# A streaming encoder step: first unit of the out-projection transposed among the value and gate blocks, two tanh buffers, one more mixer step, first sums of the up projection queued behind out-projection operands

## Chip, core and metric

One core of a Trainium2 chip runs the whole program. The metric is the device time in microseconds of one launch. Engine names are those of the profile: PE multiplies matrices (PEld is its weight load), DVE and ACT do elementwise work, POOL is the general engine, SP issues most DMAs.

## The reference

One layer of a hybrid encoder takes 1024 new frames of one stream (the prompt) and 32 frames of a running stream (the samples), each of 1024 channels. Three groups of heads mix along time, each with a state that is carried from chunk to chunk of 64 frames; then come an out-projection and a feed-forward part with a causal convolution.

```python
proj = xn @ w_in                      # xn = rms_norm(x); 15 pieces
# GLA, 6 heads, and HGRN2, 5 heads, per chunk of 64:
scores = jnp.einsum('bihd,bjhd,bijhd->bijh', qc, kc, decay)
o = (jnp.einsum('bijh,bjhv->bihv', scores, vc)
     + jnp.einsum('bihk,bhkv->bihv', qc * jnp.exp(b), s))
# mLSTM, 5 heads: the same with stabilised weights and a normaliser
cat = jnp.concatenate([o_a, o_b, o_c], axis=-1)   # normed per head, times a gate
h = cat @ w_out
x = x + rms_norm(h, g_mix_post)
up, buf = causal_dwconv(rms_norm(x, g_ffn_pre) @ w_up, ...)
x = x + rms_norm((gelu(gate) * val) @ w_down, g_ffn_post)
```

All of it is in fp32. The states and the convolutions' last rows are outputs too.

## The kernel before

Every fp32 product is made of three matmuls on operands that are split into a high and a low half (`mm3`, L100 to L103): high by high, high by low, low by high. So each operand has an "h" tile, which ACT casts, and an "l" tile, which the DVE subtracts.

*In-projection.* Frames come in three groups of 384, 384 and 288 (256 of the prompt and the 32 samples). For each group `inproj` first makes feature blocks (tiles pf, 24 matmuls each), then value and gate blocks (tiles pv). In the last group a block of 256 columns is made in two halves of 128 (`vg_across`, L446 to L474): ACT copies each half out of PSUM (vf, L468), and PE transposes it back (pb, L455). Gates go through `vg_store` (L415 to L432): tanh on ACT into the tile vth (L113), one or two DVE operations (L427, L429), a multiply on POOL (L431), and a DMA.

*Mixers.* A unit is 128 frames; unit 8 is the 32 samples. `mixer` (L719 to L1027) is a generator with NMIX = 11 steps: it loads the unit's queries and keys (qkb, L729), makes the decayed queries qe on ACT (L812), the operands Qz and Ld of the scores on the DVE, the scores on PE (sc, L717), puts them into P (L805), and sums og, oh, om and oi on PE (all L717; mi are small sums); the DVE brings these into the tile cat (L990), POOL multiplies it with the gate (L992), and it is stored (L1025). og needs P, oi comes after om, and each PSUM bank is free again when its cat is made.

*Interleaving.* `merge(main, nmain, nside)` runs the main generator and after each of its steps as many steps of the mixers as keep both in proportion. So NMIX and nmain shift every mixer step among the main work. A scheduler then orders the instructions of each engine; `tc.high_priority` pulls an instruction ahead and `tc.issue_after` holds one behind another. Each engine runs its own list in order.

*Out-projection.* `outproj(u)` (L1054 to L1187) loads a unit's cat (tile ct), transposes it (ctp, L1074), splits it (ch on ACT L1078, cl on DVE L1079), multiplies it with the weights (zp), squares and copies the result on ACT (L1101, L1102), norms it, adds the residual and transposes it for the next stage (fxt). `out_weights` casts the eight rows of w_out (woh on ACT, L107 and L1048; wol on the DVE, L110 and L1050). They come through a ring of seven tiles of which six are loaded first. `pipeline` (L1191) runs the units 0, 1, 2, 3, 8, 4, 5, and the mixers of 8, 6 and 7 run beside it. Units 6 and 7 follow by hand, beside the start of the up projection.

*Up projection.* `col_operands` (L1211 to L1243) splits sums of blocks of the normed activations xg0 into B21h, B21l, B11h and so on (ACT L1221, DVE L1222). The weights come as wu0r and wu22r, and ACT casts them into A_0h and S_0h.

## Time and profile before

| | us |
|---|---|
| median of three runs | 1377.05 |
| their range | 1376.05 to 1380.32 |
| the profiled execution | 1379.03 |
| its span in the trace | 1377.3 |
| PE busy | 1313.3 |
| DVE busy | 1031.8 |
| ACT busy | 703.9 |
| POOL busy | 325.6 |

A row of the timeline gives the start, the duration, the engine, the line, the operation with its output and inputs, and in brackets how long the engine stood idle before it and what ended that. The granted clock of PE is a column of the view by stretches (1.00 is full speed).

### The profile page before, as it was taken

How to read it: one execution, taken by the hardware profiler on the slowest of the kernel's cores; microseconds unless marked ns; L12 is line 12 of the kernel's file. 1: busy time of each engine (PE TensorE's matmuls, PEld its weight loads, DVE VectorE, ACT ScalarE, POOL GpSimd, SP SyncE). 2: the span in 40 equal slices, each digit the busy share in tenths (PEclk: the TensorE clock that was granted, in tenths of full speed). 3: DMA queues.
4: the chain of work that ended last, by engine and by line, in shares of the span. 5: the costliest groups of instructions: out<-in, count | busy, mean ns of one | idle time of the engine just before them, and what ended most of it. 6: DMA issues, size and time to landing. Idle time of an engine off the chain costs nothing.

```text
span 1377.3 us, 29190 instructions
## 1 busy us (share of the span) xinstructions
PE 1313.3 (95%) x11472; PEld 1194.7 (87%) x11472; DVE 1031.8 (75%) x1916; ACT 703.9 (51%) x1368; POOL 325.6 (24%) x529
## 2 busy tenths in 40 slices
PE   6999999998998989997989999999999999999996
PEld 5999989998887877866879999999999997678885
DVE  4786469668597577796778888888888875499566
ACT  4555556554474554443575455455555445454552
POOL 5532403145122064133111112121121110010005
PEclk9999999999999999999999999999999999999998
DMA  9599869785888844534323565645474239744435
GB/s 343 203 321 359 288 235 299 267 281 188 273 256 309 303 147 161 155 114 151 110 77 110 170 165 135 163 129 163 111 182 126 81 114 390 290 153 136 146 106 123
DMA packets 125825, 269.72 MB, mean 196 GB/s; under 512 B 24007, under 2 KB 59367, under 8 KB 125607
## 3 DMA queue, kind: packets, MB, share of 16 engines
q1 hardware_dynamic: 111959, 245.43, 52.2%
q0 software_dynamic: 8928, 18.09, 7.2%
q10 hardware_dynamic: 4800, 4.33, 0.9%
q8 instruction: 90, 1.47, 0.4%
q14 instruction: 48, 0.39, 0.1%
HBM read 206.72 MB, written 86.18 MB: 213 GB/s over the span
## 4 chain that ended last, share of the span: by engine, by line
PE 72%; DVE 11%; DMA 7%; ACT 5%; issue 2%; POOL 2%; SPq 1%; ACTq 0%; DVEq 0%; POOLq 0%
PE pux L103 5%; PE pux L101 5%; PE pux L102 5%; PE puw L101 3%; PE puw L102 3%; PE puw L103 3%; PE pv L101 3%; PE pv L103 3%; PE q L101 3%; PE pv L102 3%; PE q L102 3%; PE q L103 3%; PE x L101 2%; PE x L102 2%; PE x L103 2%
## 5 line engine op out<-in xcount | busy, mean ns | idle before, releaser
L1368 DVE SCALAR_TENSOR_TENSOR y<-uu,fconv_sb,y 128x1060 f32<-128x1060 f32 x88 | 116.2, 1320 | 37.3 <-ACT y L1366 36.9
L1304 ACT COPY c<-pux 128x272 f32<-128x272 f32 (+1 forms) x132 | 49.4, 376 | 48.3 <-PE pux L103 47.6
L101 PE MATMUL zp<-woh,ch 128*128 128x512 f32 (+1 forms) x144 | 60.5, 422 | 4.8 <-ACT ch L1078 2.8
L101 PE MATMUL pv<-wt_0h,xh 128*128 128x256 f32 (+2 forms) x195 | 57.6, 296 | 5.2 <-ACT xh L321 2.8
L103 PE MATMUL zp<-woh,cl 128*128 128x512 f32 (+1 forms) x144 | 59.0, 410 | 1.9 <-DVE cl L1079 1.9
L1366 ACT ACTIVATE y<-uu,fconv_sb 128x1060 f32<-128x1060 f32 x44 | 56.0, 1273 | 7.9 <-POOL uu L1362 6.8
L102 PE MATMUL zp<-wol,ch 128*128 128x512 f32 (+1 forms) x144 | 58.9, 409 | 0.0
L1365 POOL COPY fhalo<-uu 128x2 f32<-128x2 f32 x44 | 16.5, 376 | 178.9 <-DVE uu L1309 178.7
L103 PE MATMUL pv<-wt_0h,xl 128*128 128x256 f32 (+2 forms) x195 | 56.0, 287 | 0.2 <-DVE xl L322 0.2
L102 PE MATMUL pv<-wt_0l,xh 128*128 128x256 f32 (+2 forms) x195 | 56.0, 287 | 0.1
L103 PE MATMUL pv<-wt_1h,xl 128*128 128x256 f32 (+2 forms) x195 | 56.1, 288 | 0.0
L101 PE MATMUL pv<-wt_1h,xh 128*128 128x256 f32 (+2 forms) x195 | 55.9, 287 | 0.0
L102 PE MATMUL pv<-wt_1l,xh 128*128 128x256 f32 (+2 forms) x195 | 55.7, 286 | 0.0
L1544 POOL TENSOR_TENSOR gss<-gss 128x1 f32<-128x1 f32 (+1 forms) x9 | 8.4, 930 | 185.1 <-ACT gjk L1537 185.1
L220 POOL TENSOR_SCALAR hrs<-hss 128x5 f32<-128x5 f32 (+3 forms) x27 | 9.7, 358 | 175.4 <-DVE hss L988 174.7
L805 DVE COPY_PREDICATED P<-masks_sb,sc 128x352 f32<-128x352 int32 (+3 forms) x53 | 37.8, 714 | 11.6 <-PE sc L717 10.9
L101 PEld LDWEIGHTS pv<-wt_0h,xh 128*128 128x128 f32 (+1 forms) x195 | 36.8, 189 | 7.1 <-ACT xh L321 3.5
L431 POOL TENSOR_TENSOR vg<-vth,gh 128x256 f32<-128x256 f32 (+1 forms) x36 | 29.1, 810 | 58.5 <-DVE vth L427 36.6
L221 POOL TENSOR_TENSOR hrs<-hrs,mhalf 128x5 f32<-128x5 f32 (+3 forms) x27 | 39.7, 1471 | 2.2
L827 ACT ACTIVATE x<-x 128x256 f32<-128x256 f32 (+1 forms) x44 | 17.9, 406 | 43.3 <-DVE x L825 36.1
L101 PEld LDWEIGHTS zp<-woh,ch 128*128 128x128 f32 (+1 forms) x144 | 27.4, 190 | 12.5 <-ACT ch L1078 3.0
L992 POOL TENSOR_TENSOR cat<-cat,gt 128x320 f32<-128x320 f32 (+3 forms) x27 | 31.7, 1174 | 26.4 <-DVE cat L990 26.3
(1714 smaller groups left out, 5351.3 us busy)
## 6 DMA issues: line engine op xcount, KB each, us to landing
wrP<-in_w_dn SPq DMA_DIRECT2D x27, 512.0 KB, 4.0
h_d<-y SPq DMA_DIRECT2D x22, 530.0 KB, 3.2
ht<-h_d SPq DMA_DIRECT2D x22, 530.0 KB, 9.8
wt_0r<-in_w_tok SPq DMA_DIRECT2D x21, 512.0 KB, 7.1
wt_1r<-in_w_tok SPq DMA_DIRECT2D x21, 512.0 KB, 6.1
ws_d<-in_w_dn POOLq DMA_DIRECT2D x20, 512.0 KB, 9.1
wrP<-ws_d SPq DMA_DIRECT2D x20, 512.0 KB, 3.9
wt_0l<-lt_d SPq DMA_DIRECT2D x14, 512.0 KB, 5.7
```

The lines of the kernel that those rows point to most:

```text
L101: pe.matmul(ps, lh[0], rh[0], start=first, stop=False, **kw)
L102: pe.matmul(ps, lh[0], rh[1], start=False, stop=False, **kw)
L103: return pe.matmul(ps, lh[1], rh[0], start=False, stop=last, **kw)
L221: pool.tensor_tensor(out, out, mhalf[:n, :cols], op=ALU.pow)
L431: pool.tensor_tensor(o[:n], th[:n], gh[:n, c0:c0 + 256], op=ALU.mult)
L805: dve.copy_predicated(dst, mk.broadcast_to([n, 11, *mk.shape[2:]]), src)
L827: act.activation(xv[:, :, 0, :], xv[:, :, 0, :], AF.Exp, scale=-1.0)
L992: pool.tensor_tensor(cat[:n, c0:c0 + 64 * nh], cat[:n, c0:c0 + 64 * nh], gt[:n, c0:c0 + 64 * nh], op=ALU.mult)
L1304: kept[name] = act.copy(t, ps)
L1365: behind["POOL"] = pool.tensor_copy(fhalo[:, j, :], u[:, NCOL - 2:NCOL])
L1366: act.activation(y, u, AF.Identity, scale=fconv[:, j, 2:3], bias=fconv[:, j, 3:4])
L1368: dve.scalar_tensor_tensor(y, uu[i][:, s:s + NCOL], fconv[:, j, s:s + 1], y, op0=ALU.mult, op1=ALU.add)
```

## The change

1. Unit 0's transposes and halves are started inside `vg_across`, after the first half of the last block, with tiles of their own in a pool pc0; `pipeline` no longer starts unit 0, and unit 1's cat is loaded after unit 0's transposes.
2. vth has two buffers, in the pool of the in-projection, which the weights of the out-projection take over later.
3. ACT's copy vf is made with high priority.
4. The mixer has one more step ahead of og (NMIX 12, and `merge` gets 25 instead of 26 for the pipeline).
5. xg0 is allocated later, in the memory that pc0 leaves.
6. B21's halves of the first block are held behind the last ch and cl of unit 7.

Numbers of instructions stay nearly the same on every engine. What the order shows:

ACT at the start of the out-projection, before. ch with 6872 and 6881 are unit 0's halves, vth with 6836, 6842 and 6848 the last tanhs, qe is unit 6's.

```order
L468 COPY vf_6745<-pv_7_1_6801 128x288
L113 ACTIVATE vth_7_6836<-pb_7_6827 128x256
L107 CAST woh<-wor_5736 128x1024
L107 CAST woh<-wor_5738 128x1024
L1078 CAST ch_6872<-ctp_6867 128x512
L113 ACTIVATE vth_7_6842<-pb_7_6827 128x256
L1078 CAST ch_6881<-ctp_6876 128x512
L1048 CAST woh<-wor_5740 128x1024
L1048 CAST woh<-wor_5742 128x1024
```

And of the change, the same place, from the same copy vf on:

```order
L469 COPY vf_6748<-pv_7_1_6822 128x288
L113 ACTIVATE vth_7_6857<-pb_7_6848 128x256
L113 ACTIVATE vth_7_6863<-pb_7_6848 128x256
L113 ACTIVATE vth_7_6869<-pb_7_6849 32x256
L819 ACTIVATE qe_7397<-qkb_7336,cf_sb 128x128 x4
L995 ACTIVATE sq_0_7234<-og_7189 32x384
L107 CAST woh<-wor_5736 128x1024
L107 CAST woh<-wor_5738 128x1024
L1056 CAST woh<-wor_5740 128x1024
```

ch of unit 0 has moved ahead of this piece, all tanhs and qe of unit 6 stand ahead of the first cast of the weights, and so does a square of og of unit 8 (sq). Before, qe stood behind the last cast.

PE at unit 6's om and oi in the change (zp with 7773 is the second half of unit 3; 24 of its products stand ahead of om):

```order
L103 MATMUL zp_7773<-woh,cl_7665 128x512
L724 MATMUL om_7800<-vm_157,w_7405 64x65 x10
L724 MATMUL oi_7801<-C_0_7747,mqz 64x65
L724 MATMUL oi_7801<-C_1_6498,mqz 64x65
L724 MATMUL oi_7801<-C_0_7747,mqz 64x65
```

Before, the same om stood among the products of unit 8's second half (zp with 8284), 30 products after og:

```order
L103 MATMUL zp_8284<-woh,cl_7847 32x512
L717 MATMUL om_7770<-vm_157,w_7375 64x65 x10
L101 MATMUL zp_8284<-woh,ch_7846 32x512
L102 MATMUL zp_8284<-wol,ch_7846 32x512
L103 MATMUL zp_8284<-woh,cl_7847 32x512
```

There 18 products of zp_8284 and the four transposes of the next unit stood between om and oi; now nothing does.

ACT at the end of unit 5 in the change (zp with 8485 and 8512 are unit 5's halves, ch with 8567 and 8576 unit 6's, with 8612 and 8620 unit 7's):

```order
L1115 COPY z_8484<-zp_8485 128x512
L1238 CAST B11h_8766<-xg_8628 128x1088
L107 CAST A_0h<-wu0r 128x512 x2
L1114 ACTIVATE z_8484,oss_8483<-zp_8512 128x512
L107 CAST A_0h<-wu22r 128x512
L1115 COPY z_8484<-zp_8512 128x512
L1086 CAST ch_8567<-ctp_8562 128x512
L1086 CAST ch_8576<-ctp_8571 128x512
L1086 CAST ch_8612<-ctp_8607 128x512
```

Before, at the same place:

```order
L987 ACTIVATE sq_11_8373<-hn_8365 128x320
L1221 CAST B21h_8758<-xg_6864 128x1088
L1101 ACTIVATE z_8485,oss_8484<-zp_8513 128x512
L1221 CAST B11h_8762<-xg_6864 128x1088
L1102 COPY z_8485<-zp_8513 128x512
L1078 CAST ch_8568<-ctp_8563 128x512
L1078 CAST ch_8577<-ctp_8572 128x512
L1078 CAST ch_8613<-ctp_8608 128x512
L107 CAST A_0h<-wu0r 128x512 x2
```

B21h is gone from the front and follows the last ch; the three casts A_0h now stand ahead of unit 6's ch.

The diff:

```diff
...
     cols_of, dcs_of = {}, {}
     HSET = (2, 0, 4, 5)
     VGD = (lambda b, h: b > 0, lambda b, h: True, lambda b, h: True)
-    pws, wo_raw, ring = ExitStack(), [], []
+    pws, pcs, wo_raw, ring, p2, wo, opened = ExitStack(), ExitStack(), [], [], [], [], []
     NRING, CT0 = 7, 6
 
     ct_of, xr_of, tail, xlate, mixed = {}, {}, [], {}, set()
...
                 act.dma_start(v_d[t:t + n, 256 * blk:256 * blk + 256], o[:n])
                 return
             c0 = 256 * (blk - 4)
-            th = mx.tile([128, 256], F32, tag="vth", name=f"vth{u}_{blk}", bufs=1)
+            th = p1.tile([128, 256], F32, tag="vth", name=f"vth{u}_{blk}", bufs=2)
             ia = tanh(th[:n], ps[:n, :256], 0.5)
             ns = min(max(704 - c0, 0), 256)
             if ns:
...
                     ps = psb.tile([128, T], F32, tag="big", name=f"pv{g}_{blk}_{e}")
                     for k in range(8):
                         mm3(ps, [w[:, 128 * e:128 * e + 128] for w in ws[k]], (xh[:, k, :], xl[:, k, :]), k == 0, k == 7)
-                    act.copy(fs[e], ps)
+                    with tc.high_priority(offset=AHEAD):
+                        act.copy(fs[e], ps)
+                    if blk == blks[-1] and not e:
+                        first = outproj(RING[0])
+                        next(first)
+                        next(first)
+                        opened.append(first)
                     if before and not e:
                         back(*before)
                     yield
...
                     load_cat(0)
                 wo_raw.append(ring[0](f"wor{k}"))
                 sp.dma_start(wo_raw[k], a["w_out"][k])
+            p2.append(pcs.enter_context(tc.tile_pool(name="pc0", bufs=1, side="left")))
         if sl:
             yield from vg_across(range(1, 8))
             return
...
             if last_pair:
                 put(0, sd[:n].unsqueeze(2).broadcast_to([n, 11, cl]))
             yield
+        yield
 
         og = psm.tile([128, 6, 64], F32, tag="o", name=f"og{u}", bufs=2)
         oh = psm.tile([128, 5, 64], F32, tag="o", name=f"oh{u}", bufs=2)
...
     lev_index = {16: 0, 8: 1, 4: 2, 2: 3, 1: 4, 0: 5}
 
 
-    def outproj_setup(p2):
-        woh = p2.tile([128, 8, 1024], F32R, name="woh")
-        wol = p2.tile([128, 8, 1024], F32R, name="wol")
-        gm = p2.tile([128, 1024], F32, name="gm")
+    def outproj_setup():
+        woh = p2[-1].tile([128, 8, 1024], F32R, name="woh")
+        wol = p2[-1].tile([128, 8, 1024], F32R, name="wol")
+        gm = p2[-1].tile([128, 1024], F32, name="gm")
         sp.dma_start(gm, a["grows"][0:1, :].broadcast_to([128, 1024]))
         return gm, woh, wol
 
...
             yield
 
 
-    def outproj(p2, W, u):
-
-        gm, woh, wol = W[:3]
+    def outproj(u):
+
         n = 128 if u < 8 else DEC
         t0 = 128 * u
         load_cat(u)
-        if u in RING:
+        if u in RING[1:]:
             load_cat((RING + (6,))[RING.index(u) + 1])
         ct = ct_of[u]
         chs = []
...
             for k in range(4):
                 c = 512 * hf + 128 * k
                 pe.transpose(ps[:, k, :n], ct[:n, c:c + 128], ident[:n, :n])
-            ch = p2.tile([128, 4, 128], F32R, tag="ch", name=f"ch{u}{hf}", bufs=3)
-            cl = p2.tile([128, 4, 128], F32R, tag="cl", name=f"cl{u}{hf}", bufs=3)
+            own = f"{hf}" if u == RING[0] else ""
+            ch = p2[-1].tile([128, 4, 128], F32R, tag="ch" + own, name=f"ch{u}{hf}", bufs=1 if own else 3)
+            cl = p2[-1].tile([128, 4, 128], F32R, tag="cl" + own, name=f"cl{u}{hf}", bufs=1 if own else 3)
             with tc.high_priority(offset=AHEAD):
                 ins = (act.copy(ch[:, :, :n], ps[:, :, :n]),
                        dve.tensor_tensor(cl[:, :, :n], ps[:, :, :n], ch[:, :, :n].bitcast(F32), op=ALU.subtract))
             if u == RING[0]:
                 halves[:] = ins
+            if u == 7:
+                kept["ch"], kept["cl"] = ins
             chs += [(ch[:, k, :n], cl[:, k, :n]) for k in range(4)]
             if u in RING:
                 yield
         if u not in RING:
             yield
+        if u == RING[0]:
+            load_cat(RING[1])
         if u in RING:
             load_res(u)
-        ss = p2.tile([128, 4], F32, tag="oss", name=f"oss{u}", bufs=2)
+        gm, woh, wol = wo[:3]
+        ss = p2[-1].tile([128, 4], F32, tag="oss", name=f"oss{u}", bufs=2)
         cs = [slice(512 * hf, 512 * hf + 512) for hf in range(2)]
 
         def bank(hf):
...
 
             pss = [bank(hf) for hf in range(2)]
             for k in range(8):
-                next(W[3])
+                next(wo[3])
                 for hf in range(2):
                     product(pss[hf], hf, k)
             z = ring[0](f"z{u}")
...
             zt = z[:, :8 * n].rearrange("p (k n) -> p k n", n=n)
         else:
             s = u > 5
+            if not s and 0 not in xlate:
+                pcs.close()
+                xlate[0] = p3s.enter_context(tc.tile_pool(name="p3", bufs=1, side="right")).tile([128, 8, 2, SUBS[0][1]], F32, name="xg0")
             o = fcol(u) - HW - SUBS[s][0] - 2
             zt = xlate[s][:, :, 1, o:o + n]
         for hf in range(2):
...
     def pipeline(gens):
 
 
-        next(gens[0])
-        next(gens[0])
-        yield
         for i, x in enumerate(gens):
             after = gens[i + 1:i + 2]
             next(x)
...
             h = p.tile([128, 4, n], F32R, name=f"{name}h{s}")
             l = p.tile([128, 4, n], F32R, name=f"{name}l{s}")
             res[name] = h, l
-            act.copy(h, src)
-            return dve.tensor_tensor(l, src, h.bitcast(F32), op=ALU.subtract)
+            with ExitStack() as late:
+                if s == 0 and name == "B21":
+                    late.enter_context(tc.issue_after(kept["ch"].ins))
+                    late.enter_context(tc.issue_after(kept["cl"].ins))
+                act.copy(h, src)
+                return dve.tensor_tensor(l, src, h.bitcast(F32), op=ALU.subtract)
 
         halves("B21", q["B21"])
         halves("B11", q["B11"])
...
         return chain_of(*[mixer(u, g, c) for (u, c) in us[-1:] + us[:-1]]) if us[-1][0] == 8 else \
             chain_of(*[mixer(u, g, c) for (u, c) in us])
 
-    NMIX, NIN = 11, 12 + 2 + 24
+    NMIX, NIN = 12, 12 + 2 + 24
 
     for g in range(3):
         xs_ = norm_tiles(g)
...
         side.append(mixers(g))
     p1s.close()
     p2s = ExitStack()
-    p2 = p2s.enter_context(tc.tile_pool(name="p2", bufs=1, side="right"))
-    wo = outproj_setup(p2)
-    wo += (out_weights(wo),)
+    p2.append(p2s.enter_context(tc.tile_pool(name="p2", bufs=1, side="right")))
+    wo += outproj_setup()
+    wo.append(out_weights(wo))
     p3s = ExitStack()
 
-    x0 = p3s.enter_context(tc.tile_pool(name="p3", bufs=1, side="right")).tile([128, 8, 2, SUBS[0][1]], F32, name="xg0")
-    xlate[0] = x0
     n0, n1 = SUBS[0][1], SUBS[1][1]
     smp = DEC // 2
-    firsts = [outproj(p2, wo, u) for u in RING]
-    merge(pipeline(firsts), 26, 3 * NMIX + 2)
+    firsts = opened + [outproj(u) for u in RING[1:]]
+    merge(pipeline(firsts), 25, 3 * NMIX + 2)
     pump(1000)
-    last = [outproj(p2, wo, u) for u in (6, 7)]
+    last = [outproj(u) for u in (6, 7)]
     for x in (last[0], last[0], last[1]):
         next(x)
+    if 0 not in xlate:
+        pcs.close()
+        xlate[0] = p3s.enter_context(tc.tile_pool(name="p3", bufs=1, side="right")).tile([128, 8, 2, SUBS[0][1]], F32, name="xg0")
+    x0 = xlate[0]
     sp.dma_start(x0[:, :, 0, :], xn_d[:, :, 0:n0])
     sp.dma_start(x0[:, :, 1, :smp], xn_d[:, :, HW:HW + smp])
     sp.dma_start(x0[:, :, 1, smp:smp + 128], xn_d[:, :, fcol(4):fcol(5)])
```

## The prediction

> **What bounds the kernel now.** The page first: PE is busy almost the whole span.
>
> ```profile
> PE 1313.3 (95%) x11472; PEld 1194.7 (87%) x11472; DVE 1031.8 (75%) x1916; ACT 703.9 (51%) x1368; POOL 325.6 (24%) x529
> ```
>
> Only 64.0 us (1377.3 less 1313.3) are open on PE, so an edit that adds no products can win little. I then read what PE waited for between 480 and 710 us, where most of the edits lie (us in total, times, longest).
>
> ```profile
> PE zp L101 <- ACT ch L1078: 2.8, 1, 2.8
> PE sc L717 <- DVE Qz L839: 1.5, 1, 1.5
> PE pb L455 <- DVE vth L427: 1.3, 1, 1.3
> PE ctp L1074 <- ACT vth L113: 0.8, 1, 0.8
> PE pv L101 <- DVE vth L427: 0.8, 2, 0.6
> ```
>
> No wait is long, and three groups answer to the edits: the tanh buffer (pb, pv, ctp), the operands of unit 6 (ch), and the waits of mixers. The table by stretches adds the clock: in the first 8 us of the out-projection it is half, so products cost twice.
>
> ```profile
> 514.00:522.00 8.00, 2.51 (x4) 1.33 (x4) 0.50 0.96 347
> 645.00:654.00 9.00, 3.83 (x24) 2.68 (x23) 6.53 (x8) 6.28 (x11) 4.13 (x5) 0.89 0.56 173
> ```
>
> The columns are busy PE and PEld (the second row all five engines), then the clock and the DMA share; the first row counts L102 alone, of which only the clock is used. In the second, PE works 3.83 of 9 us: that is the densest loss in the kernel.
>
> **Term A, two tanh buffers.** The tanh tile had one buffer, so a new tanh waits until POOL has read the last one. The trace of this tile and PE's rows:
>
> ```profile
>   POOL vg L431: 21.5, 15
> 338.39 0.40 PE L101 MATMUL pv<-wt_0h,xh 128*128 128x282 f32 x1 [1.35 <-ACT vth L113]
> 493.05 0.38 PE L455 MATMUL pb<-ident,vf 128*32 128x128 f32 x2 [1.27 <-DVE vth L427]
> ```
>
> ACT stood 21.5 us in 15 waits for POOL, but of that only 1.35, 1.3 and 0.8 us came through to PE (3.4 us), and 0.8 more to ctp. A second buffer takes away exactly this wait. ACT's high priority for the vf copy costs no instruction; it matters only where PE waits for the copy, and I count it at nothing, bounds 1 us either way. What is late next is POOL's own multiply, which is not faster.
>
> **Term B, one more step in each mixer.** The order puts one block of 24 products more between a mixer's last sum (mi) and og for unit 3, whose og waited:
>
> ```profile
> 316.33 0.92 PE L717 MATMUL og<-v,P 64*64 64x64 f32 x24 [2.81 <-DVE P L805]
> 506.03 0.29 PE L102 MATMUL pv<-xl,wt_1h 128*128 128x288 f32 x1
> 506.16 0.29 PE L103 MATMUL pv<-xh,wt_1l 128*128 128x288 f32 x1
> ```
>
> Products of this kind start 0.13 us apart, so 24 of them are 3.1 us, more than the 2.81. The price is that blocks elsewhere in the mixer lose cover; no row shows such a wait, so I bound it by the same 2.8 us of loss. A and B together offer 6.2 us. Because each stage still has the DVE behind it, I take half, **−3.1 us**, with bounds −7 and +3.
>
> **Term C, the start of the out-projection.** T is the end of the value and gate products, 506.4 us by the row above. Unit 0's eight transposes and its four halves stand ahead of T now. That alone would let unit 0 begin early. But its first product also needs the cast weights woh, and the order puts qe of unit 6 ahead of all eight casts on ACT. ACT's rows before, with the load of qkb on SP, the first product, and the last scores, og and oh of unit 8:
>
> ```profile
> 509.80 0.42 PE L717 MATMUL sc<-cf_sb,x 128*32 128x11 f32 x8
> 517.19 1.48 PE L717 MATMUL og<-v,P 32*32 32x64 f32 x12
> 531.47 0.86 PE L717 MATMUL og<-S,qz 128*32 128x64 f32 x12
> 532.16 0.72 PE L717 MATMUL oh<-S,qz 128*32 128x64 f32 x10
> 509.08 1.98 ACT L107 CAST woh<-wor 128x1024 fp32r<-128x1024 f32 x2
> 513.42 4.83 ACT L1048 CAST woh<-wor 128x1024 fp32r<-128x1024 f32 x5
> 516.52 0.84 SPq L729 DMA_DIRECT2D qkb<-qkb_d  x2
> 522.50 1.28 ACT L812 ACTIVATE qe<-qkb,cf_sb 128x128 f32<-128x128 f32 x4 [3.05 <-DMA qkb<-qkb_d]
> 513.93 0.76 PE L101 MATMUL zp<-woh,ch 128*128 128x512 f32 x1 [1.04 <-issue]
> 532.86 0.69 DVE L1079 TENSOR_TENSOR cl<-ctp,ch 128x512 fp32r<-128x512 f32 x1 [9.24 <-ACT ch L1078]
> ```
>
> Before, the casts begin at T+2.7 and the first product at T+7.5. After, SP issues qkb when unit 8's scores are over, T+3.8 by the first row, say T+4. From issue to qe took 6.0 us (516.52 to 522.50), so qe runs from T+10 to T+11.3; one square and one cast of 1.0 us (1.98 for two) follow, and the first product stands near T+13: 5.5 us later. Against that stand og and oh of unit 8, 3.1 us of PE (1.48, 0.86 and 0.72), which the order puts ahead of the first product and thus into this hole. Unit 0's products stay spread by the casts and the DVE's subtractions (five took 5.77 us), and the eighth cast, behind a load which is now queued after qkb, may hold its last six. I take **+2 us**. The DVE's idle 9.24 us before 532.86 is what unit 6's mixer may use, since its qkb is now there early: if all its work falls there the start wins 3 us. The upper end is a late load: qe of unit 7 waited 9.4 us for its qkb, and with that much more for qkb, and some 4.6 us more for the eighth cast's load behind it, the end is +16. The wait, in the view of ACT's waits:
>
> ```profile
> ACT qe L812 <- DMA qkb<-qkb_d: 12.5, 2, 9.4
> ```
>
> PE will idle 6 us there, and the clock goes with it: in the row of 514 to 522 it was 0.50 after idle pieces of about 1 us. The Trainium skill, "TensorE: Matmul & The Clock Gate", Part 1: The HAM clock gate, says that the array returns to half speed after an idle window of about 3.4 us and recovers after a busy one. By that rule one more window at half speed may follow, an estimate of 1.7 us more; this trace halves the clock with far smaller gaps, so the hole does not have to add any, and the sum goes without it.
>
> **Term D, units 6 and 7 among the products.** Both mixers stand half a unit to one and a half earlier among the products (og half a unit, the first scores more). Before, unit 7 paid at its end:
>
> ```profile
> 626.54 0.91 PE L717 MATMUL og<-v,P 64*64 64x64 f32 x24 [0.93 <-DVE P L805]
> 628.71 0.76 PE L717 MATMUL oh<-S,qz 128*64 128x64 f32 x20
> 632.35 0.80 PE L717 MATMUL om<-vm,w 64*64 64x65 f32 x20 [1.83 <-DVE cat L990]
> 631.74 0.56 DVE L990 TENSOR_TENSOR cat<-og,hrs 128x384 f32<-128x384 f32 x1 [0.68 <-POOL hrs L221]
> 539.00 2.44 DVE L781 TENSOR_TENSOR qz<-qkb,eb 32x256 f32<-32x256 f32 x6
> 633.27 0.49 DVE L990 TENSOR_TENSOR cat<-oh,hrs 128x320 f32<-128x320 f32 x1 [0.18 <-POOL hrs L221]
> ```
>
> Now 22 products stand ahead of unit 7's og and 23 ahead of its om, some 5 us each, so these 2.76 us go. For unit 6 it is worse: oi follows om directly, and the DVE has the decay, four query products and the solver's operands of unit 7 ahead of the cat that frees oi's bank. In the rows above that cat ends at 633.76, 4.3 us after the last product of og and oh (628.71 and 0.76). The query products alone took 2.44 us for unit 6; with the rest I estimate 4, which makes 8.3. The cover is 24 products 0.23 us apart (5.5 us, by two rows of the next fence) and om, 0.80: 6.3 us. So oi waits 2.0 us: D is 2.0 − 2.8 = **−0.8 us**, bounds −2.8 and +6 (unit 7's qkb as late as above).
>
> **Term E, unit 6's operands ahead of B21's halves.** ACT, SP and PE at the end of unit 5:
>
> ```profile
> 644.59 0.39 PE L102 MATMUL zp<-wol,ch 128*128 128x512 f32 x1
> 644.82 0.40 PE L103 MATMUL zp<-woh,cl 128*128 128x512 f32 x1
> 647.30 1.10 ACT L1221 CAST B21h<-xg 128x1088 fp32r<-128x1088 f32 x1 [3.56 <-POOL cat L992]
> 648.89 1.09 ACT L1221 CAST B11h<-xg 128x1088 fp32r<-128x1088 f32 x1
> 650.36 1.57 ACT L1078 CAST ch<-ctp 128x512 fp32r<-128x512 f32 x3
> 651.79 1.18 ACT L107 CAST A_0h<-wu0r 128x512 fp32r<-128x512 f32 x2
> 647.30 0.33 SPq L1251 DMA_DIRECT2D wu0r<-in_w_up  x1
> 651.01 0.50 PE L101 MATMUL zp<-woh,ch 128*128 128x512 f32 x1 [2.76 <-ACT ch L1078]
> 653.69 0.80 PE L103 MATMUL zp<-woh,cl 128*128 128x512 f32 x1 [1.94 <-DVE cl L1079]
> ```
>
> B21h waits 3.56 us for unit 7's last cat, and ch stands behind it. With ch ahead and the mixer over sooner, the waits of 2.76 and 1.94 us go, and with them the clock's loss in this stretch, 0.11 of 9 us or 1.0 us: **−5.7 us**; bounds 0 and −6.7 (as much again for the clock behind it). B21 itself comes later, but B11 and 48 products stand before it. The first weights of the up projection (A_0h) now stand ahead of ch, which is the weak point below. The later tile of xg0 moves its three loads no further than unit 5; I count nothing, bound 1 us.
>
> **Sum.** −3.1 + 2 − 0.8 − 5.7 = −7.6 us on the profiled execution's 1379.03 us (span 1377.3, and 1.7 around it), that is 1371.4. This execution lies 2.0 us above the median of 1377.05, which gives 1369.4; I round to a forecast of **1370 us**.
>
> **The rivals.**
>
> *The load ahead of the casts makes it slower.* ACT works in its order, so each us that unit 6's qkb comes late goes on the first product. Term C at +16 instead of +2 gives +6.4: 1379.0 + 6.4 − 2.0 = 1383 us. It is slower by more than 0.3% (4.1 us, about what a measurement here can tell from no change) once C is above 13.7, that is, with unit 0's products held 11.7 us longer than I take. For it: the 9.4 us wait, and a DMA share of 0.96 in 514 to 522. Against: the load is issued ahead of the others.
>
> *The tail does not pay.* A_0h, ahead of ch on ACT, waits for a load issued at 647.30 that let it run at 651.79, 1.4 us after the ch it would now hold. If that load is issued no earlier, E is 0: −1.9, and 1379.0 − 1.9 − 2.0 is 1375 us, no change that can be told. Against: unit 7 is over earlier, and the load was issued as its last cat ended.
>
> *All of it pays.* A and B in full (−6.2), C at −1, D at −2.8, E at −6.7: −16.7, so 1360 us. For it: DVE's 9.24 us of idle time. Against: the hole on ACT.
>
> *It does not do what it says*, ch staying behind B21h and the transposes behind pb, which would give 1377 us: the order shows both moved, so it gets no chance of its own.
>
> **How the numbers follow.** The forecast 0.46, the late load 0.18, the tail that does not pay 0.23, all of it 0.13. Faster is the first and the last, 0.59; the same 0.23; slower 0.18. The forecast's own range is 1364 to 1373. The range for 8 in 10, 1361 to 1381, reaches into both outer cases and leaves some 0.1 out at either end.
>
> **What would show it.** In the changed profile: ACT's tanh no longer released by POOL; og of unit 3 without its wait; a first out-projection product near T+13, with ACT idle before qe for the load; om and og of unit 7 without waits, and oi of unit 6 with one; ch of unit 6 within 2 us of its transposes. A first product after T+20, A_0h idle ahead of ch, or new waits of pf and pv in the groups 1 and 2 would make the prediction wrong.

## The result and the profile after

| us | before | change |
|---|---|---|
| median, six runs each, same chip | 1376.6 | 1387.25 |
| range | 1375.79 to 1380.41 | 1385.26 to 1388.81 |
| profiled execution | 1379.03 | 1385.26 |
| its span | 1377.3 | 1383.5 |

The change is **slower**, by 0.7%: 1.0069 times the time before (95% interval 1.0052 to 1.0086). The forecast was 1370 us with a range up to 1381, so sign and range are both wrong. The profiled pair differs by 6.2 us, less than the medians, since the profiled execution of the change is the fastest of its six. One later run of the kernel before lasted 1595.67 us at a mean clock of 0.751 and is left out of every comparison.

The engines' totals on the page of the changed kernel:

```profile
PE 1320.0 (95%) x11472; PEld 1199.3 (87%) x11472; DVE 1032.6 (75%) x1916; ACT 706.5 (51%) x1368; POOL 325.1 (23%) x529
```

PE has as many matmuls as before and is busy 6.7 us longer (1320.0 against 1313.3). Its idle time is 63.5 us, against 64.0 before. So the change did not make PE wait longer; it made PE **work longer at the same work**. The view by stretches shows where. I cut both traces at the same events: the second half block of group 2, T (the end of value and gate products), the end of unit 0's 48 products, and the ends of units 5 and 7. The columns are the window, its length, busy PE, PEld, DVE, ACT and POOL with their instructions, the clock, the DMA share and GB/s. First the kernel before:

```profile
338.40:506.50 168.10, 155.47 (x2034) 140.66 (x2036) 121.52 (x314) 90.34 (x217) 43.79 (x66) 0.98 0.78 260
506.50:530.80 24.30, 22.35 (x155) 16.65 (x154) 16.20 (x32) 11.57 (x19) 6.29 (x9) 0.79 0.64 211
530.80:644.90 114.10, 108.92 (x1252) 85.92 (x1251) 90.93 (x201) 48.50 (x120) 39.71 (x56) 0.99 0.44 137
644.90:679.70 34.80, 29.63 (x137) 24.05 (x136) 25.91 (x31) 18.65 (x38) 6.66 (x10) 0.90 0.43 136
```

And the same stretches of the change:

```profile
336.80:512.00 175.20, 162.74 (x2028) 147.62 (x2030) 122.97 (x331) 92.47 (x221) 43.05 (x64) 0.94 0.75 250
512.00:541.00 29.00, 24.39 (x209) 18.87 (x209) 22.86 (x47) 13.27 (x24) 20.01 (x16) 0.82 0.53 163
541.00:654.00 113.00, 107.34 (x1210) 82.69 (x1209) 83.88 (x182) 47.57 (x114) 33.38 (x52) 1.00 0.46 144
654.00:686.50 32.50, 28.81 (x127) 22.82 (x126) 24.31 (x29) 18.13 (x37) 3.69 (x8) 0.89 0.37 125
```

Up to group 2 the change has won 1.6 us (336.8 against 338.4). Then it loses 7.1 in group 2 and 4.7 at the start of the out-projection, and wins 1.1 in the middle, 2.3 at the tail and 0.6 behind it: 6.2 in all. Group 2 is the first thing to read. PE's idle time there is the same (168.10 less 155.47 is 12.6; 175.20 less 162.74 is 12.5), but the clock fell from 0.98 to 0.94. What the clock withholds, (1 − clock) times the length, grew from 3.4 to 10.5 us: the whole 7.1. In the clock's own records PE is at half clock for 6.8 us of this stretch before, and for 20.5 us in the change.

What happens there shows at PE's longest waits. The first row is of the kernel before, the other four of the change: two of scores, one of pb and one of the last pv.

```profile
441.66 1.33 PE L455 MATMUL pb<-ident,vf 128*128 128x128 f32 x5 [3.22 <-ACT vf L468]
335.23 1.13 PE L724 MATMUL sc<-Qz,Ld 64*64 64x64 f32 x58 [1.90 <-DVE Qz L846]
421.55 0.67 PE L724 MATMUL sc<-Qz,qkb 64*64 64x64 f32 x32 [2.89 <-DVE P L812]
443.83 0.90 PE L455 MATMUL pb<-ident,vf 128*128 128x128 f32 x3 [2.81 <-ACT vf L469]
497.10 0.40 PE L101 MATMUL pv<-xh,wt_0h 128*128 128x288 f32 x1 [2.17 <-ACT vf L469]
```

The wait of pb for vf is not new: it was 3.22 us before, with 6.8 us of half clock around it, and is 2.81 us in the change, with 6.8 us again. New are the other three, and with them the half clock from 338, 423 and 498 us (3.4, 6.8 and 3.4 us long). The stretches around the waits at 421.55 and 497.10, same columns as above:

```profile
419.90:423.30 3.40, 1.75 (x69) 1.74 (x69) 3.36 (x10) 1.67 (x4) 0.93 (x3) 0.93 0.82 218
423.30:430.10 6.80, 6.80 (x63) 6.20 (x64) 6.03 (x11) 1.42 (x3) 0.00 (x0) 0.53 0.78 228
495.00:498.40 3.40, 1.30 (x8) 1.30 (x9) 2.41 (x10) 1.43 (x4) 0.94 (x2) 0.93 0.26 58
498.40:501.80 3.40, 3.40 (x18) 3.40 (x16) 1.75 (x3) 0.37 (x1) 3.40 (x5) 0.56 0.00 0
```

Here a stretch of 3.4 us in which PE works for only 1.75 or 1.30 us is followed by 6.8 or 3.4 us in which it is busy throughout, at about half clock. Half clock for 3.4 us costs 1.7 us of work, so such a wait costs its own length and 1.7 or 3.4 us more.

At the start of the out-projection, ACT, SP, POOL and PE of the change:

```profile
516.25 0.37 ACT L113 ACTIVATE vth<-pb 32x256 f32<-32x256 f32 x1 [1.35 <-POOL vg L431]
520.41 1.28 ACT L819 ACTIVATE qe<-qkb,cf_sb 128x128 f32<-128x128 f32 x4 [3.79 <-DMA qkb<-qkb_d]
521.97 1.97 ACT L107 CAST woh<-wor 128x1024 fp32r<-128x1024 f32 x2
515.41 0.85 SPq L736 DMA_DIRECT2D qkb<-qkb_d  x2
518.24 0.73 POOL L431 TENSOR_TENSOR vg<-vth,gh 32x256 f32<-32x256 f32 x1
523.05 1.22 PE L101 MATMUL zp<-woh,ch 128*128 128x512 f32 x2 [0.35 <-ACT woh L107]
540.16 0.50 PE L102 MATMUL zp<-wol,ch 128*128 128x512 f32 x1 [2.07 <-DVE wol L1058]
```

qe holds the first cast to 521.97 (T+10.0), the first product stands at T+11.1, and the eighth cast holds PE for 2.07 us more. POOL's last gate multiply, now at 518.24, ends at T+7.0.

At the tail, the groups ACT, DVE, SP and PE:

```profile
655.41 1.14 ACT L107 CAST A_0h<-wu0r 128x512 fp32r<-128x512 f32 x2 [4.00 <-DMA wu0r<-in_w_up]
658.86 0.59 ACT L1086 CAST ch<-ctp 128x512 fp32r<-128x512 f32 x1 [0.73 <-PE ctp L1081]
656.06 1.29 DVE L110 TENSOR_TENSOR A_0h<-wu0r,A_0h 128x512 fp32r<-128x512 f32 x2 [3.33 <-ACT A_0h L107]
657.27 1.28 DVE L1199 TENSOR_TENSOR z<-fxt,gcols_sb 128x512 f32<-128x512 f32 x2
650.16 0.34 SPq L1268 DMA_DIRECT2D wu0r<-in_w_up  x1
658.02 1.66 PE L1081 MATMUL ctp<-ident,ct 128*128 128x128 f32 x8 [2.80 <-DVE z L1199]
661.61 0.80 PE L103 MATMUL zp<-woh,cl 128*128 128x512 f32 x1 [0.89 <-DVE cl L1087]
```

ACT stands idle 4.00 us ahead of A_0h for a load issued at 650.16. Its lower half stands on the DVE right behind it, and ahead of z, whose bank PE needs for unit 6's transposes: PE waits 2.80 us there. The wait for ch is gone, as forecast; another, of the same length, has come one step earlier.

### The profile page after: what moved, and what is told of

Read it like the earlier page. It is cut to its first block, busy times and chain, and to the rows that moved or that the text cites. A ratio compares the mean times of both kernels' runs of the same rounds, so it can differ in the third digit from the quotient of the medians.

```text
span 1383.5 us, 29228 instructions
## 1 busy us (share of the span) xinstructions
PE 1320.0 (95%) x11472; PEld 1199.3 (87%) x11472; DVE 1032.6 (75%) x1916; ACT 706.5 (51%) x1368; POOL 325.1 (23%) x529
## 3 DMA queue, kind: packets, MB, share of 16 engines
q8 instruction: 90, 1.47, 0.4%
## 4 chain that ended last, share of the span: by engine, by line
PE 73%; DVE 13%; DMA 6%; ACT 4%; issue 2%; POOL 1%; SPq 1%; DVEq 0%; POOLq 0%; ACTq 0%
PE pux L101 4%; PE pux L102 4%; PE pux L103 4%; PE pv L101 4%; PE pv L103 3%; PE pv L102 3%; PE puw L102 3%; PE puw L101 3%; PE puw L103 3%; PE q L101 3%; PE q L102 3%; PE q L103 3%; PE x L101 2%; PE x L102 2%; PE x L103 2%; PE sc L724 2%
## 5 line engine op out<-in xcount | busy, mean ns | idle before, releaser
L220 POOL TENSOR_SCALAR hrs<-hss 128x5 f32<-128x5 f32 (+3 forms) x27 | 13.3, 492 | 187.8 <-DVE hss L996 187.1
L1000 POOL TENSOR_TENSOR cat<-cat,gt 128x320 f32<-128x320 f32 (+3 forms) x27 | 36.0, 1337 | 31.1 <-DVE cat L998 30.1
L103 PEld LDWEIGHTS pv<-wt_0h,xl 128*128 128x128 f32 (+1 forms) x195 | 37.3, 191 | 0.9 <-DVE xl L322 0.8
L102 PEld LDWEIGHTS pv<-wt_0l,xh 128*128 128x128 f32 (+1 forms) x195 | 37.2, 191 | 0.6 <-POOL wt_0l L110 0.5
L101 PEld LDWEIGHTS pv<-wt_1h,xh 128*128 128x128 f32 (+1 forms) x195 | 37.0, 190 | 0.5 <-issue 0.2
```

The source lines that it names most:

```text
L101: pe.matmul(ps, lh[0], rh[0], start=first, stop=False, **kw)
L102: pe.matmul(ps, lh[0], rh[1], start=False, stop=False, **kw)
L103: return pe.matmul(ps, lh[1], rh[0], start=False, stop=last, **kw)
L220: pool.tensor_scalar(out, ss, 1.0 / width, eps, op0=ALU.mult, op1=ALU.add)
L1000: pool.tensor_tensor(cat[:n, c0:c0 + 64 * nh], cat[:n, c0:c0 + 64 * nh], gt[:n, c0:c0 + 64 * nh], op=ALU.mult)
```

## The experiments

A ratio stands against runs of the kernel before on the same chip, with its 95% interval. Where a mean over all runs of the kernel before is used, it is that of the 97 taken beside the experiments, 1378.7 us. Beside each time I use what the clock withheld: (1 − mean clock) times span, averaged over a kernel's runs. For the kernel before that is 22.6 us, and 1356.1 remain. This measure also counts half clock in which PE stands idle, as at the very end of the kernel.

The first question was which part costs. **Four kernels with one part each**, on the kernel before. The extra mixer step alone:

```diff
+        yield
         og = psm.tile([128, 6, 64], F32, tag="o", name=f"og{u}", bufs=2)
...
-    NMIX, NIN = 11, 12 + 2 + 24
+    NMIX, NIN = 12, 12 + 2 + 24
```

> The kernel before with only the extra mixer step (NMIX 12). Theory 1, the shifted interleaving makes new waits of 1 to 3 us on PE, each followed by half-clock windows: slower by 4 to 9 us (1381 to 1386), with more half-clock pieces before 510 us than the 4 of before. Theory 2, the loss is the hole at the start of the out-projection that early unit-0 work and qe ahead of the casts make: within 2 us of before (1375 to 1379).

1378.53 us, 1.0000 (0.9985 to 1.0014): nothing. The wait of 2.81 us for og of unit 3 is gone from its trace, as term B says, but others stand in its place, above all 3.55 us of a pv for the tanh tile (0.57 before).

The early start of unit 0 alone, with the late tile xg0, one tanh buffer and 11 steps:

```diff
+                    if blk == blks[-1] and not e:
+                        first = outproj(RING[0])
+                        next(first)
+                        next(first)
+                        opened.append(first)
...
-        next(gens[0])
-        next(gens[0])
-        yield
```

> The changed kernel with the one-buffer tanh tile, the vf copy without priority, NMIX 11 and B21 not held back: only unit 0's early transposes and the later xg0 are left. Theory 1: within 2 us of before. Theory 2: slower by 3 to 6 us (1380 to 1383), with the first product of the out-projection 3 us or more later behind the end of the gate products than before's 7.5 us.

1387.08 us, 1.0064 (1.0045 to 1.0083). The loss is not at the start: the first product is at T+6.0, earlier than before. It is in the middle (122.0 us for 114.1) and in group 2 (174.0 for 168.1), where PE waits longer for vf (3.22 us before) and, new, for P:

```profile
444.56 1.26 PE L455 MATMUL pb<-ident,vf 128*128 128x128 f32 x5 [4.97 <-ACT vf L468]
575.12 1.08 PE L723 MATMUL sc<-Qz,qkb 64*64 64x64 f32 x32 [4.02 <-DVE P L811]
```

The second tanh buffer alone:

```diff
-            th = mx.tile([128, 256], F32, tag="vth", name=f"vth{u}_{blk}", bufs=1)
+            th = p1.tile([128, 256], F32, tag="vth", name=f"vth{u}_{blk}", bufs=2)
```

> The kernel before with only the two tanh buffers in the in-projection's pool. Theory 1 (the extra step is the cause): 0 to 4 us faster (1373 to 1377), the tanh's waits for POOL gone. Theory 3, the second buffer's place makes the weight casts wait for POOL's last multiply: slower by 2 to 4 us, first product 2 us or more later.

1386.05 us, 1.0054 (1.0042 to 1.0066). Again the middle is long, 126.3 us for 114.1, with the clock lower and waits between the units' products:

```profile
574.99 0.91 PE L717 MATMUL og<-v,P 64*64 64x64 f32 x24 [2.25 <-DVE P L805]
586.75 0.85 PE L717 MATMUL oi<-C,mqz 128*64 128x65 f32 x20 [2.42 <-DVE cat L990]
```

Each of these two loses about as much as the whole change, so their losses do not add up. The order of B21's halves alone:

```diff
-            act.copy(h, src)
-            return dve.tensor_tensor(l, src, h.bitcast(F32), op=ALU.subtract)
+            with ExitStack() as late:
+                if s == 0 and name == "B21":
+                    late.enter_context(tc.issue_after(kept["ch"].ins))
+                    late.enter_context(tc.issue_after(kept["cl"].ins))
+                act.copy(h, src)
+                return dve.tensor_tensor(l, src, h.bitcast(F32), op=ALU.subtract)
```

> The kernel before with only B21's halves held behind unit 7's operands. If the price of unit 6's operands behind B21h was the 4.7 us of waits and 1 us of clock: 1371 to 1373. If another wait takes their place (unit 7's last cat, the weights' load): within 2 us of before, 1375 to 1378.

1377.10 us, 0.9997 (0.9980 to 1.0013): no gain that can be told. The two waits shrink from 2.76 and 1.94 us, and no further than this:

```profile
650.85 0.50 PE L101 MATMUL zp<-woh,ch 128*128 128x512 f32 x1 [1.91 <-ACT ch L1078]
653.37 0.79 PE L103 MATMUL zp<-woh,cl 128*128 128x512 f32 x1 [1.78 <-DVE cl L1079]
```

Both parts that lose, lose in the middle among the mixers of 6 and 7. So a first theory was that these mixers had come **too early** among the products. **Three kernels set them later** again: on the change (after_late), on vth_alone and on early_alone.

```diff
-            want = (i + 1) * nside // nmain
+            want = max(i + 1 - lag, 0) * nside // nmain if i < nmain - 1 else nside
...
+    BEHIND = {6: (39, 47, 59, 63, 73), 7: (79, 90, 95, 95, 95)}
+        line[0] = zpi[min(BEHIND[u][i], len(zpi) - 1)] if u in BEHIND and BEHIND[u][i] else None
```

> The changed kernel, but the mixers of units 6 and 7 follow two main steps later in the out-projection, and their scores, og and om are queued on PE behind the same products as before (first scores of unit 6 behind 144 products instead of 60, og behind 192 instead of 144, om behind 215 instead of 168). Theory M, the mixers that stand too early among the products make PE wait (og 2.1, oi 1.8 us and what follows at half clock): 1380 to 1384, no wait of og or oi over 1 us between the starts of the second and seventh unit's products. Theory S, the late start and the waits in group 2 are the loss: 1385 to 1388, as the change.

1389.84 us, 1.0090 (1.0069 to 1.0110).

> The kernel before with two tanh buffers alone, and the mixers of units 6 and 7 three main steps later, behind the products as before (og of unit 6 behind 178 instead of 144). Theory M: the 7.5 us that the buffers alone cost are back, 1376 to 1380. If the buffers cost by themselves (casts behind POOL): 1383 to 1387, unchanged.

1381.96 us, 1.0032 (1.0014 to 1.0050).

> Only unit 0's early transposes, with the mixers of units 6 and 7 two main steps later (first scores of unit 6 behind 144 instead of 96 products, og behind 178 instead of 157). Theory M: the wait of 4.0 us for P at the third scores of unit 6 and its half clock go, 1380 to 1383. Theory S: unchanged, 1386 to 1388.

1385.72 us, 1.0062 (1.0045 to 1.0079). The theory falls for the change and for the early start: only the tanh kernel gets part of its loss back. early_late is the one kernel here whose loss is not the clock's (22.4 us withheld, like before, but 1362.8 remain).

**Four kernels undo one part** of the change each. Without the extra step:

```diff
-        yield
...
-    NMIX, NIN = 12, 12 + 2 + 24
+    NMIX, NIN = 11, 12 + 2 + 24
```

> The changed kernel without the extra mixer step. If the extra step costs nothing, as alone: 1385 to 1389. If it makes the waits of group 2 (scores for P 2.9 us, the gate blocks for their weights 2.1 us): 1380 to 1383, with the end of the gate products 4 us or more earlier than the change's 512.

1384.49 us, 1.0057 (1.0042 to 1.0073). Without the early start (the removed lines of early_alone's diff back), and without the second tanh buffer:

```diff
-                        first = outproj(RING[0])
-                        next(first)
-                        next(first)
-                        opened.append(first)
```

> The change without unit 0's early transposes (and with xg0 as before). If the second tanh buffer alone is enough for the loss: 1383 to 1387, clock 0.977 to 0.980. If it needs the early transposes: 1376 to 1380.

1384.19 us, 1.0040 (1.0019 to 1.0062).

```diff
-            th = p1.tile([128, 256], F32, tag="vth", name=f"vth{u}_{blk}", bufs=2)
+            th = mx.tile([128, 256], F32, tag="vth", name=f"vth{u}_{blk}", bufs=1)
```

> The change with the one-buffer tanh tile. If the early transposes alone are enough: 1384 to 1388, clock 0.977 to 0.980. If the two losses add: 1379 to 1382 here, and the change's own 9 us would be their sum.

1384.96 us, 1.0057 (1.0039 to 1.0075). Without the priority of the vf copy:

```diff
-                    with tc.high_priority(offset=AHEAD):
-                        act.copy(fs[e], ps)
+                    act.copy(fs[e], ps)
```

> The change without the vf copy's priority. If the new wait of a gate block for that copy (2.2 us at 497) and the half-clock stretch behind it come from the priority: 1383 to 1385 and no such wait. If not: 1385 to 1389, unchanged.

1385.80 us, 1.0045 (1.0028 to 1.0061). All four stay slower than before, and each wins at most some 3 us. No single one of these edits holds the loss. Both edits that lose, taken out together, leave a kernel with the extra step, the vf priority and B21's order:

```diff
+                    with tc.high_priority(offset=AHEAD):
+                        act.copy(fs[e], ps)
...
+        yield
...
+                if s == 0 and name == "B21":
+                    late.enter_context(tc.issue_after(kept["ch"].ins))
+                    late.enter_context(tc.issue_after(kept["cl"].ins))
```

> The kernel before with the vf copy's priority, the extra mixer step and B21 held back, but neither unit 0's early transposes nor the second tanh buffer. If these two edits carry the loss: 1375 to 1379, granted clock as before (0.983 to 0.985). If the three others lose together: 1381 or more.

1377.72 us, 0.9985 (0.9967 to 1.0002), and once more, since the interval touches 1:

> The kernel without the two costly edits once more, since its first interval, 0.9967 to 1.0002 of before, just reaches no change. If its lower rest of 3 us (time less clock loss) is real: 1 to 4 us below before again. If not: within 1 us.

1378.16 us, 0.9993 (0.9980 to 1.0006). That is the kernel before again, no more.

**The clock as the cause.** The losses have one thing in common, with early_late as the exception:

| mean over a kernel's runs, us | time | withheld by the clock | the rest |
|---|---|---|---|
| before (97 runs) | 1378.7 | 22.6 | 1356.1 |
| change | 1387.1 | 30.7 | 1356.4 |
| early_alone | 1387.2 | 30.7 | 1356.5 |
| vth_alone | 1385.9 | 30.5 | 1355.4 |
| b21_alone | 1377.2 | 23.5 | 1353.7 |
| no_early | 1384.0 | 30.4 | 1353.6 |
| no_vth | 1385.0 | 27.2 | 1357.8 |
| after_no_yield | 1384.5 | 27.9 | 1356.7 |
| after_no_vf | 1385.8 | 28.7 | 1357.1 |
| after_late | 1389.5 | 31.2 | 1358.2 |
| early_late | 1385.2 | 22.4 | 1362.8 |

The change's 8.4 us are 8.1 us of clock and 0.3 of all the rest. For the profiled pair alone the same measure gives 24.7 and 28.0 us, only 3.3 of the 6.2, mostly because before has more half clock at its idle end. Counted only while PE works, half the time at half clock is 18.0 us before and 23.7 in the change: 5.7 of the 6.2. In b21_alone and no_early the rest is 2.4 us lower than before, so something there does win; in no_early the clock takes three times that back. The table alone could still be a coincidence of two columns, so I put waits into the kernel before, in a part that the change doesn't touch (the products p5 of the later stages). A transpose that waits for a chain of 0 to 6 copies on POOL stands ahead of 15 blocks; nothing of the computation is left out.

```diff
+                if hops is not None:
+                    t = PROBE[0]
+                    with tc.high_priority(offset=10 * AHEAD):
+                        act.copy(t, x[:, :128])
+                        for i in range(hops):
+                            pool.tensor_copy(t, t)
+                        hold.enter_context(tc.issue_after(pe.transpose(w[:, :128], t, ident).ins))
+                product(w, "p5", W, X, True, True)
...
```

> The kernel before with 15 waits put into PE's stream in the up projection, where it has almost none: in each of 15 blocks PE transposes a copy of a sum that it has just made, into a bank that the next product overwrites, and the copy takes 0, 1, 2, 4 or 6 further copies on POOL. Outputs are not changed. Theory G, a wait of about 1.4 us or more inside one 3.4 us stretch of the clock's own grid puts the next stretch at half speed: waits under 1 us are followed by full speed, most waits over 2 us by 3.4 us at half speed, long ones by 6.8, and the time grows by the waits plus 1.7 us for each stretch. Rival, the clock falls for another reason (only the small matmuls of the mixers, or the load in general): no stretch at half speed between 740 and 1180 us, and the time grows by the waits alone.

1416.38 us, 1.0279 (1.0259 to 1.0299); of this only the clock is of use, since the rest is the waits and work put in. One of the waits of 0.7 us, and four of the five of about 2 to 3 us:

```profile
758.58 0.33 PE L1330 MATMUL puw<-ident,probe 128*128 128x128 f32 x1 [0.70 <-ACT probe L1327]
850.55 0.33 PE L1330 MATMUL puw<-ident,probe 128*128 128x128 f32 x1 [2.84 <-POOL probe L1329]
941.24 0.48 PE L1330 MATMUL puw<-ident,probe 128*128 128x128 f32 x1 [2.99 <-POOL probe L1329]
1057.16 0.33 PE L1330 MATMUL puw<-ident,probe 128*128 128x128 f32 x1 [2.19 <-POOL probe L1329]
1080.67 0.46 PE L1330 MATMUL puw<-ident,probe 128*128 128x128 f32 x1 [1.90 <-POOL probe L1329]
```

The stretches behind these five, in the same order:

```profile
758.60:762.00 3.40, 3.40 (x27) 3.40 (x28) 2.19 (x5) 1.49 (x3) 1.82 (x4) 1.00 0.63 192
852.50:855.90 3.40, 3.40 (x19) 3.40 (x18) 1.89 (x2) 0.67 (x2) 1.21 (x1) 0.57 1.12 214
941.30:944.70 3.40, 3.40 (x17) 3.40 (x18) 2.67 (x3) 0.84 (x2) 0.00 (x0) 0.57 1.11 198
1057.30:1060.70 3.40, 3.40 (x28) 3.40 (x28) 2.87 (x3) 1.10 (x3) 0.13 (x1) 1.00 0.93 157
1081.20:1084.60 3.40, 3.40 (x18) 3.40 (x18) 3.33 (x3) 0.65 (x2) 0.70 (x1) 0.57 0.83 152
```

PE is busy throughout in all five. Behind the waits of 2.84, 2.99 and 1.90 us it has 0.57 of the clock and does 17 to 19 matmuls where it otherwise does 27 or 28; behind 0.70 and, once, behind 2.19 it has the full clock. Of the five longest waits put in, four were followed by such a stretch (the one not shown is of 2.89 us, at 967.05); the kernel before has no half clock anywhere between 713 and 1369 us. In the means the clock withholds 29.7 us, 7.1 more than before; four stretches at 1.7 us make 6.8. So one wait of 2 to 3 us is enough for it, which is what the theory needs; that it does not always do it is shown too. All four stretches are 3.4 us long; why some in the change are 6.8 us or more, the probe does not show.

Is the pattern of the change its own, or a chance of one execution? The changed kernel again, unaltered:

> The change once more, beside the two, for the place of its half-clock stretches. If they belong to its waits, the stretches behind the waits of 2 us and more (scores for P in group 2, vf, og of unit 6, unit 6's transposes) are at half speed again, and the mean clock is 0.976 to 0.980; if they fall anywhere, their places differ and the clock may be as before, 0.983.

1387.38 us, 1.0052 (1.0035 to 1.0070). Its group 2:

```profile
337.60:515.40 177.80, 165.23 (x2024) 150.51 (x2026) 122.69 (x329) 92.73 (x221) 43.03 (x64) 0.92 0.73 246
```

The same waits (sc 1.91 us at 335.96 and 2.90 at 423.65, pv 2.17 at 500.54), and half clock again from 338, 423, 502, 522 and 662, where the first profile had it from 338, 423, 498, 518 and 658; that of 423 is 3.4 us longer. Others move: half clock around the vf wait at 444 in the first, and here at 454 behind a wait of 3.69 us for wt_0l, which was 0.82 us in the first; from 362, 597 and 1191 here alone; from 703 and 710 there alone.

**The start.** Is qe's load what holds the first product? qe and eb of unit 6 behind the last cast:

```diff
-        with tc.issue_after(outs[0].ins) if outs else ExitStack():
+        with tc.issue_after(outs[0].ins) if outs else ExitStack(), tc.issue_after(wcast[-1].ins) if u == 6 else ExitStack():
...
-        with tc.issue_after(vcopies[8].ins) if u == 0 else ExitStack():
+        with tc.issue_after(vcopies[8].ins) if u == 0 else tc.issue_after(wcast[-1].ins) if u == 6 else ExitStack():
```

> The change with unit 6's decay and qe queued on ACT behind the last cast of the weights, so that the casts do not wait for unit 6's load. If the hole at the start (first product 11 us behind the gate products instead of 7.5) is what the change loses: first product within 9 us and 1381 to 1384. If the loss lies in the waits of group 2 and of the mixers: 1385 to 1389.

1388.25 us, 1.0066 (1.0046 to 1.0087): no gain. The first product is at T+11.4. ACT's next in the queue takes qe's place:

```profile
521.05 0.48 ACT L996 ACTIVATE sq<-og 32x384 f32<-32x384 f32 x1 [4.93 <-PE og L725]
521.43 1.97 ACT L107 CAST woh<-wor 128x1024 fp32r<-128x1024 f32 x2
```

og's square now holds the casts to the same time. So the load is not the only thing that ends there; to take it away is not enough.

**The tail.** A_0h and its fellows behind unit 6's ch and cl, everything else as in the change:

```diff
+            if u == 6:
+                kept["ch6"], kept["cl6"] = ins
...
-        for name, src in (("A12", a12), ("A11", a11), ("A22", a22)):
-            res[name] = weight_halves(f"{name}_{f}h", src)
+        with ExitStack() as hold:
+            if not f:
+                hold.enter_context(tc.issue_after(kept["ch6"].ins))
+                hold.enter_context(tc.issue_after(kept["cl6"].ins))
+            for name, src in (("A12", a12), ("A11", a11), ("A22", a22)):
+                res[name] = weight_halves(f"{name}_{f}h", src)
```

> The change with the first weights of the up projection (A_0h and their low parts) queued behind unit 6's operands on ACT and DVE. If A_0h's wait of 4.0 us for its load held the transposes and ch of unit 6: the wait of the transposes for DVE (2.8 and 1.6 us in the two profiles of the change) goes, and with its half-clock stretch 2 to 4 us: 1383 to 1385. If the wait only moves to the first sums of the up projection: 1386 to 1388.

1381.05 us, 1.0018 (1.0003 to 1.0032). The stretch of units 6 and 7 in the view by stretches, and from the timeline ACT's ch and A_0h and PE's transposes and first product with cl:

```profile
654.00:681.50 27.50, 26.32 (x126) 21.04 (x125) 25.23 (x30) 18.21 (x38) 3.56 (x8) 1.00 0.42 135
```

```profile
655.44 1.56 ACT L1086 CAST ch<-ctp 128x512 fp32r<-128x512 f32 x3 [0.57 <-PE ctp L1081]
656.88 1.16 ACT L107 CAST A_0h<-wu0r 128x512 fp32r<-128x512 f32 x2
654.75 1.09 PE L1081 MATMUL ctp<-ident,ct 128*128 128x128 f32 x8 [0.35 <-DVE z L1201]
657.42 0.50 PE L103 MATMUL zp<-woh,cl 128*128 128x512 f32 x1 [0.60 <-DVE cl L1087]
```

27.5 us, for 32.5 in the change and 34.8 before; the waits of 2.80 and 0.89 us are 0.35 and 0.60, and the clock is full. PE's list is the same as in the change up to 669 us, and only ACT and the DVE work in another order there; behind it four transposes stand five products later, and from 715 to 760 us some products of the up projection change places. This one edit is worth 5.7 us of the change's loss (1387.1 less 1381.4 in the means), of which 3.9 is the clock (30.7 to 26.8). What is left of the loss is 0.18%.

## Why the prediction was wrong

The sum gave −7.6 us for the profiled execution; it measured +6.2. The miss of 13.8 us by terms, from the stretches:

- **A and B**, −3.1 expected, +5.5 measured (−1.6 ahead of group 2, +7.1 in it). What the two terms said would go is gone: POOL ends 7.4 us of idle time for the tanh tile instead of 21.5, no PE instruction waits for it, and og of unit 3 doesn't wait. But others came: 1.92 us of a pf block for q (at 229) and 1.90 of scores for Qz ahead of group 2, 2.89 for P and 2.17 for vf in it. The forecast had named new waits of pf and pv there as a sign of being wrong. PE's idle time in group 2 stayed the same, and the clock fell. Term A's "what is late next is POOL's own multiply" was too short a list. The eight transposes of unit 0 also moved into this stretch.
- **C**, +2 expected, +4.7 measured, with the first product at T+11.1 for T+13. The place of the hole was right, and half clock lasts 10.2 us there in both kernels. PE's idle time grew by 2.7 us (1.95 to 4.61), part of it the eighth cast, which held PE 2.07 us; the rest of the 4.7 is more work in this stretch (209 matmuls for 155). And the load was not the only cause, as after_hold shows.
- **D**, −0.8 expected, −1.1 measured, but this agreement is luck. oi of unit 6 waits 1.83 us for 2.0 expected, and om and og of unit 7 don't wait, as forecast. But og of unit 6 waits 2.14 us for P, which no term had, and PE's idle time in the middle grew by 0.5 us. What won is a stretch of 3.4 us at half clock, from 604, behind a wait of 1.47 us for Qz: it is gone, and that is 1.7 us.
- **E**, −5.7 expected, −2.3 measured. This lies between the forecast and the rival "the tail does not pay", given 0.23, and went the rival's way: A_0h waits 4.00 us for its load. It got there by a way I hadn't drawn: not ch on ACT, but z on the DVE, behind A_0h's lower half, held PE. after_a0 shows that with A_0h behind ch the tail wins 7.3 us (34.8 less 27.5), so the term was there to be had, and the order took two thirds of it.
- Behind the tail, −0.6, not in the sum.

The rows for D, the first of the kernel before, the others of the change:

```profile
603.05 1.14 PE L717 MATMUL sc<-Qz,Ld 64*64 64x64 f32 x64 [1.47 <-DVE Qz L839]
581.55 0.92 PE L724 MATMUL og<-v,P 64*64 64x64 f32 x24 [2.14 <-DVE P L812]
593.64 0.80 PE L724 MATMUL oi<-C,mqz 128*64 128x65 f32 x20 [1.83 <-DVE cat L998]
```

The **step that failed** is the price of A and B. The forecast bounded the new waits of the mixers by 2.8 us, since no row showed one, and priced every wait by its own length, with nothing for the clock behind it. In group 2 PE's idle time is 12.5 us (12.6 before), but half clock grew from 6.8 to 20.5 us; half of that increase, 6.8 us, is nearly the whole 7.1. The forecast had noted that "this trace halves the clock with far smaller gaps" and then charged for the clock in E alone. In C, where it wrote "the sum goes without it", leaving the clock out did no harm. Over the whole kernel PE's idle time stayed at 64 us, so by that pricing the change was worth nothing; nearly all of the loss, 8.1 of 8.4 us in the means, is time at half clock. That a wait of 2 to 3 us brings a half-clock stretch is shown (stall_probe). The second step is the choice in E, between two readings of one load: it was put on the wrong side, and after_a0 shows the size.

Which edits bring the new waits can be read from the kept traces. The waits of 1.9 us for Qz at 335, of 2.9 for P at 422 and of 2.2 for vf near 499 stand in all seven profiles that have both the extra step and the second tanh buffer: the two of the change, no_early, after_no_vf, after_late, after_hold and after_a0. In the twelve others there is no such wait for Qz, at most 1.03 us for P (with the step alone) and at most 1.08 for vf. So these waits need both edits: with either taken out of the change (after_no_yield, no_vth) they are gone or down to 1.1 us, though other waits stand in their place and the kernel wins only 2 to 3 us; with the early transposes or the priority of the vf copy taken out all three stay. B21's order, which lies 150 us and more behind them, was not taken out by itself. From 336 us to the end of the gate products the seven spend 17 to 27 us at half clock, 21.5 in the mean; the twelve others 3 to 20, 11.1 in the mean.

The rival that ended slower, the late load of qkb at C, was not what made it slower: the load took 5.0 us from issue to qe, 6.0 before.

Four things stay open. early_alone and vth_alone each lose 0.5 to 0.6%, most of it in the middle stage, where the whole change loses nothing; why two edits that each shift the mixers' order there cancel was not settled by the three kernels that set the mixers later. Why the step and the buffer together make the scores wait for Qz and P was not followed further. Why wt_0l comes late in group 2, by 2.6 to 4.3 us in five of the seven profiles, was not tried. And early_late loses 6.5 us that the clock does not explain.

## What to carry to other kernels

Where PE is busy 95% of the time, don't add up waits: ask whether a moved wait leaves PE idle for some 1.6 to 2 us within one stretch of 3.4 us, and charge at least 1.7 us more for each that does. Read the mean clock of all runs beside the time; here it told in one column what the busy shares hid. Two edits can make a wait that neither makes alone, as the extra step and the second buffer did, so test pairs too. And when a cast is pulled ahead of another, look at what the new head of the queue waits for: in an in-order queue a load that is 4 us late holds all that was meant to profit.

## What the runs showed of the hardware

The clock in the records changes on a grid of 3.41 us: every stretch of full or half clock inside a kernel is a whole number of them. Over all 19 profiles I sorted the stretches of that grid at full clock by PE's idle time in them, and counted how often the next was at half clock:

| idle in a stretch, us | half clock next |
|---|---|
| under 0.9 | 10 of 6898 |
| 0.9 to 1.2 | 23 of 119 |
| 1.2 to 1.4 | 7 of 62 |
| 1.4 to 1.6 | 13 of 40 |
| 1.6 to 1.9 | 41 of 63 |
| 1.9 to 2.3 | 59 of 59 |
| 2.3 to 3.4 | 55 of 55 |

So from 1.9 us of idle time on, a little over half a stretch, the next was always at half clock, and below 1.4 us seldom. In between idle time alone does not decide it. A wait that falls across the border of two stretches can go free: the one of 2.19 us left 1.86 us idle in one and 0.33 in the next, and full clock followed. The Trainium skill, "TensorE: Matmul & The Clock Gate", Part 1: The HAM clock gate, has the window of about 3.4 us running free of the kernel; the grid here agrees. It asks for one idle window before the clock falls; here stretches with PE at work for 1.30 and 1.75 us of 3.4 were enough, and the measurement decides.

The clock also makes up much of the spread from run to run of one program: the 13 fastest of the 97 runs before (mean 1374.3 us) had 19.0 us withheld by the clock, the 13 slowest (1382.8) 25.7, that is 6.7 of the 8.5 us between them. That they differ by where the grid falls on the waits would fit, but is not shown, since only one execution of this kernel was profiled.
